# Operand addresses, two interleaved projections and the stored residual stream in a three-block kernel

## The chip, the cores and the metric

One NeuronCore of a Trainium2 chip runs the whole program. The metric is the device time of one execution in microseconds (us), as the median of several. TensorE is PE, VectorE is DVE, ScalarE is ACT, GpSimd is POOL, and SP issues most DMAs.

## The reference

Sequence 512, width 1024, float32. Two blocks run one after the other:

```
for layer in 0, 1:                                  # first block
    x += mixer(rmsnorm(x))                          # layer 0: stick-breaking + windowed heads; layer 1: latent attention
    x += swiglu(rmsnorm(x))                         # hidden 2816
x = rmsnorm(x, final_norm)
proj = rms_norm(x, ln_attn_pre) @ w_in              # second block
mix  = concat(rwkv7_mix(proj[:, :1792]), diff_attention(rest))
h = x + rms_norm(mix @ w_out)
h = h + rms_norm((gelu(conv gate) * conv val) @ w_down)
```

The product `rms_norm(x) @ w_in`, with x already the normed output of the first block, is where two of the three edits are. The second block later needs this normed x again, as the residual h.

## The kernel before

Activations lie transposed: eight tiles x0 to x7 of 128 channels by 512 tokens. Each float32 operand of a product is cut into a rounded high part and a low part (`whi`, `wlo` for weights, `xh`, `xl` for activations; `h`, `l`, `ah`, `al`, `t` in the swiglu). `mm3` makes three matmuls of them, high by high, high by low, low by high; ACT makes the high part, DVE the low one. A matmul streams its second operand against the weights loaded for it, and the weights of the next matmul are loaded beside it. The widths streamed are 512 columns, or 256 in the swiglu's gate and up products (`product`, L721), which are combined from half-size blocks.

**Where tiles lie.** The pools stand one after the other in each partition's memory. Constants end at byte 18,080, which leaves 32 modulo 128. The weight pool `wp` (raw, whi, wlo) and the activation pool `xp` (x, xh, xl) begin there, and all their tiles are multiples of 128 long, so each starts at 32 modulo 128. The work pool `wk` and all pools of a stage (attention, swiglu `ff`, second block) start at 0. The pools on the right-hand side, `po` (weights of the output projection) and `ffr` (a swiglu's extra weight tiles), start at 96. In the swiglu the weight parts rotate over three places, two in `wp` and one in `ffr`; half of the activation blocks `t` lie in `ff`, half in `xp`.

**Order.** In the swiglus the order of PE, DVE, ACT and SP is written out by hand. In the second block only PE's order is; the other engines' order is made by a planner that goes by traced order and simulated readiness.

**Start of the second block.** `bridge` makes xh and xl of each x tile once the last swiglu has added to it, and two sums of squares on ACT and POOL. PE then does the first projection (24 matmuls), the sums (`norms`, L1081), the second projection, a third, and the broadcast of the norm `rbc` (L248). `norms` also gives the vector `rf` from which the residual stream is made: `keep(ks)` multiplies x by the gain on ACT, by the broadcast norm `rkv` on POOL (L1072), and stores it to DRAM over ACT's queue (L1073), to be read back much later. The table `SLOTS` says after which half projection of which head pair t each step stands; `keep:0123` stands in the last slot of t = 0, beside `norm1` (a reciprocal root by Newton steps on tiny tiles, L228 to L234, then the ACT copy `rnb`, L1192). `late` is `norm2`, whose first step on PE is `pnb` (L1199), in the middle of the next projection. The buffers x0 to x7 are taken over by the tiles `lms` in t = 1 and t = 2.

Of the kernel before, what the change touches and what calls it, by code (L numbers as in the profile page):

```python
# [8 lines left out]
F32 = mybir.dt.float32  # L9
F32R = mybir.dt.float32r  # L10
I32 = mybir.dt.int32
AF = mybir.ActivationFunctionType
ALU = mybir.AluOpType
# [69 lines left out]
class Net:  # L83
    def __init__(self, tc, A, stack, dbg=None):
        self.tc, self.nc, self.A, self.dbg = tc, tc.nc, A, dbg or {}
        nc = self.nc
        self.cst = stack.enter_context(tc.tile_pool(name="cst", bufs=1))
        self.wp = stack.enter_context(tc.tile_pool(name="wp", bufs=3))
        self.xp = stack.enter_context(tc.tile_pool(name="xp", bufs=1))
        self.sm = stack.enter_context(tc.tile_pool(name="sm", bufs=2))  # L90
        self.wk = stack.enter_context(tc.tile_pool(name="wk", bufs=2))
        self.cv = self.cst.tile([128, A["cv"].shape[1]], F32, name="cv")
        nc.sync.dma_start(out=self.cv, in_=A["cv"])
        self.tables()
        self.ident = self.cst.tile([128, 128], F32, name="ident")
        self.ones = self.cst.tile([128, 128], F32, name="ones")
        nc.vector.memset(self.ones, 1.0)
        self.x = [self.xp.tile([128, S], F32, tag=f"x{k}", name=f"x{k}") for k in range(NT)]
        self.acc = None
        self.pb = [self.pool(stack, f"p{i}", n, PSUM) for i, n in enumerate((2, 3, 2, 1))]  # L100


    def banks(self, *ids):
# [399 lines left out]
    def project_out(self, banks, w, oh, ol, cut):  # L503
        v_, g_ = self.nc.vector, self.nc.gpsimd
        for m in range(8):
            ps = banks[0][0].tile([128, S], F32, tag=banks[0][1], name="pso")
            self.dense(ps, [self.A[w][m][:, :cut * 128]], oh, ol)
            v_.tensor_tensor(out=self.x[m], in0=self.x[m], in1=ps, op=ALU.add)
        edge = Edge(self)
        with self.tc.tile_pool(name="po", bufs=1, side="right") as pw, self.tc.manual_schedule(engines={mybir.EngineType.PE}):  # L510
            n, ws, jobs = 1024 - 128 * cut, [], []

            def part(m, ps, c, ks):
                for k in ks:
                    o = slice(128 * (k - cut), 128 * (k - cut) + 128)
                    self.mm3(ps, *[w[:, o] for w in ws[m]], oh[k][:, c], ol[k][:, c], k == cut, k == 7)

            for i, c in enumerate(HALVES):
                for m in range(8):
                    p_, n_ = banks[(8 * i + m) % len(banks)]  # L520
                    ps = p_.tile([128, S], F32, tag=n_, name="pso")[:, 0:256]
                    if not i:
                        ws.append([pw.tile([128, n], F32R, name=f"w{j}{m}") for j in "hl"])
                        self.chunk(self.A[w][m][:, cut * 128:], g_ if m in PJL else None, None, ws[m])
                    jobs.append((m, ps))
                    part(m, ps, c, range(cut, 7))

                    if not i and m < PJW:
                        continue
                    for m_, ps in jobs:  # L530
                        part(m_, ps, c, (7,))
                        v_.tensor_tensor(out=self.x[m_][:, c], in0=self.x[m_][:, c], in1=ps, op=ALU.add)
                        edge.squares(m_, i)
                    jobs = []
                    if i and m == PJN[0]:
                        edge.norm(0)
                    if i and m == PJN[1]:
                        edge.spread(0)
        return edge
# [186 lines left out]
    def ffn(self, i, edge):  # L726
        nc, A = self.nc, self.A
# [4 lines left out]
        with ExitStack() as st:  # L732
            pp = self.pool(st, "ff", 1)
            w2 = self.pool(st, "ffw", 1)
            pw = st.enter_context(self.tc.tile_pool(name="ffr", bufs=1, side="right"))
            pg = self.banks(*FFB[i])
            place = lambda n: pp.tile([128, 4, 256], F32R if n != "y" else F32, tag="a", name=n, bufs=8)
# [7 lines left out]


            y, T = [place("y") for _ in range(4)], {}

            def scaled(q):
                c = HALVES[q // 2]  # L750
# [39 lines left out]
            p1, s1, m5, u, pa, pb, cs, hq, hr, done, ws, sm, quads = ({} for _ in range(13))  # L790
# [165 lines left out]
            def ahead(n):  # L956
# [3 lines left out]
                if n + 1 < len(jobs):  # L960
# [7 lines left out]
            turn = {2: lambda: quadrant("B12", 2), 3: lambda: quadrant("B22", 3),  # L968
                    4: lambda: term("T1", lambda: y[2], lambda: y[0]), 6: lambda: term("T2", lambda: y[3], lambda: t["T1"]),
                    8: lambda: term("T3", lambda: y[3], lambda: y[2]), 13: lambda: term("T4", lambda: y[1], lambda: t["T2"])}  # L970
# [63 lines left out]
    def bridge(self, psp):  # L1034
        nc = self.nc
        gg = self.sm.tile([128, 8], F32, name="gg", bufs=1)
        nc.vector.tensor_tensor(out=gg, in0=self.col("final_norm", 0, 8), in1=self.col("ln_pre", 0, 8), op=ALU.mult)
        xh = [self.xp.tile([128, S], F32R, tag=f"xh{k}", name=f"xh{k}") for k in range(NT)]
        xl = [self.xp.tile([128, S], F32R, tag=f"xl{k}", name=f"xl{k}") for k in range(NT)]
        acc2 = self.sm.tile([128, S], F32, tag="rq", name="acc2", bufs=1)  # L1040
        for k in range(NT):
            self.prep(k, self.x[k], gg[:, k:k + 1], xh[k], xl[k])
            gf = self.col("final_norm", k)
            if k == 0:
                nc.scalar.activation(out=acc2, in_=self.x[k], func=AF.Square, scale=gf)
            else:
                t = self.wk.tile([128, S], F32, tag="sqt", name="sqt")
                nc.scalar.activation(out=t, in_=self.x[k], func=AF.Square, scale=gf)
                nc.gpsimd.tensor_add(out=acc2, in0=acc2, in1=t)
        got = {}  # L1050

        def norms():
            ps = psp.tile([128, S], F32, tag="r", name="pss")
            _, vf = self.meansq(psp, D, 1e-6, ps=ps[:, 0:4])
            self.acc = acc2
            v2, _ = self.meansq(psp, D, 0.0, ps=ps[:, 4:8])
            rf = got["rf"] = self.rsqrt(vf, [128, 4], "rf", FAST[1])
            nc.vector.tensor_tensor(out=v2, in0=v2, in1=rf, op=ALU.mult)
            nc.vector.tensor_tensor(out=v2, in0=v2, in1=rf, op=ALU.mult)
            nc.vector.tensor_scalar(out=v2, in0=v2, scalar1=1e-6, scalar2=None, op0=ALU.add)  # L1060
            r2 = self.rsqrt(v2, [128, 4], "r2", FAST[1])
            nc.vector.tensor_tensor(out=r2, in0=r2, in1=rf, op=ALU.mult)
            return r2


        def keep(ks):
            if ks[0] == 0:
                got["b"] = self.bcast(psp, got["rf"], "rkv")
                self.hsp = self.A["scratch"].tile([NT, 128, S], F32, tag="hsp", name="hsp", bufs=1)
            for k in ks:  # L1070
                nc.scalar.activation(out=self.x[k], in_=self.x[k], func=AF.Copy, scale=self.col("final_norm", k))
                nc.gpsimd.tensor_tensor(out=self.x[k], in0=self.x[k], in1=got["b"], op=ALU.mult)  # L1072
                nc.scalar.dma_start(out=self.hsp[k], in_=self.x[k])  # L1073
        return xh, xl, norms, keep

    def meansq(self, psp, dim, eps, tag="r", ps=None):
# [17 lines left out]
    def block2_attn(self):  # L1094
        nc, A = self.nc, self.A
        v_, g_, s_, t_ = nc.vector, nc.gpsimd, nc.scalar, nc.tensor
        with ExitStack() as st:
            pp = self.pool(st, "ba", 1)
# [5 lines left out]
            xh, xl, norms, keep = self.bridge(pr)  # L1104
# [34 lines left out]
            def bank(name="psr"):  # L1139
                p_, n_ = banks[npb[0] % 4]  # L1140
                npb[0] += 1
                return p_.tile([128, S], F32, tag=n_, name=name)
# [177 lines left out]
                        {"norm1": norm1, "norm2": norm2, "decays": decays}[n_](t)  # L1320

            with self.tc.manual_schedule(engines={mybir.EngineType.PE}):
                first = [bank(), bank()]
                for m in range(2):
                    self.dense(first[m], [A["w_in2"][m]], xh, xl)
                    if m == 0:
                        rc = norms()
                kr = [bank(), bank()]
                self.dense(kr[0], [A["w_in2"][6]], xh, xl)
                rbc = self.bcast(pr, rc, "rbc")  # L1330
# [102 lines left out]
            with self.tc.manual_schedule(engines={mybir.EngineType.PE}):  # L1433
# [18 lines left out]
                for hh in range(2):  # L1452
                    ps = ((pg, pv)[hh]).tile([128, 4, 4, 32], F32, tag="go"[hh], name="psi")
# [4 lines left out]
                for hh in range(2):  # L1458
                    ps = pc.tile([128, 4, 4, 32], F32, tag="c", name="psi2")
# [507 lines left out]
def constants():  # L1967
# [57 lines left out]
LAG = (2, 3)  # L2025
WP = ()

SLOTS = [["", "", "", "", "decays", "norm1 next keep:0123"],
         ["late keep:45", "turn:v keep:67", "", "within:0 within:1 norm1", "turn:bh bonus", "turn:kh within:2 within:3 next"],
         ["late", "turn:v", "", "within:0 within:1", "within:2 within:3 bonus", "turn:bh turn:kh"]]  # L2030
CUT = (5, 5)
NEWT = 1
# [25 lines left out]
```

## Time and profile before

| | us |
|---|---|
| median of 3 runs (lowest, highest) | 2031.12 (2030.57, 2034.69) |
| profiled execution | 2029.36 |
| its span | 2027.7 |
| PE busy | 1931.1 |
| DVE busy | 1350.5 |
| ACT busy | 896.7 |
| POOL busy | 428.7 |

Busy time is the time in which an engine had an instruction under way; consecutive matmuls overlap, so a matmul's own duration is longer than the distance to the next one's start. The first swiglu's products begin at 293 us, the latent attention's projections at 661 us, the second swiglu's products at 905 us, the second block's at 1269 us, those of its own feed-forward part at 1649 us.

### The profile page before, as it was taken

Reading aid. Unit: us, or ns where it says so; the run is one execution under the profiler, and the core shown is the slowest. Engines: PE = TensorE matmul, PEld = TensorE weight load, DVE = VectorE, ACT = ScalarE, POOL = GpSimd, SP = SyncE. Lnnn points to the kernel's source line nnn. Section 1 sums busy time; section 2 is a strip of 40 time slices with the busy share of each in tenths; the row PEclk is TensorE's granted clock in tenths of the full one; section 3 lists DMA queues with packets and bytes.
Section 4 is the critical chain, followed back from the end, with each engine's and each line's share of the span. In section 5 each row is a group of like instructions: output and inputs, shape, how many; then the busy total and the mean of one; then the engine's idle time right before and its main releaser. Section 6 shows DMA issues by size and latency. Waiting matters only on the chain. (4 is left out here: it accounts for less than half of the span.)

```text
span 2027.7 us, 29686 instructions
## 1 busy us (share of the span) xinstructions
PE 1931.1 (95%) x11652; PEld 1646.6 (81%) x11652; DVE 1350.5 (67%) x2287; ACT 896.7 (44%) x1538; POOL 428.7 (21%) x429
## 2 busy tenths in 40 slices
PE   9999988999999999998999999889899999999997
PEld 8766788999997777778999998668687788888886
DVE  6555568777767666567867676777958578666324
ACT  5454454444344555445434445534146445444321
POOL 2434210000002265320000002354333242111001
PEclk9998998999999999999999999989999999999998
DMA  4210142323323210033323132222111112223232
GB/s 161 99 58 7 32 155 94 128 71 117 100 75 96 73 49 27 28 116 105 123 86 132 66 104 77 84 89 69 63 53 45 62 58 98 95 94 100 89 95 70
DMA packets 58123, 169.56 MB, mean 84 GB/s; under 512 B 6304, under 2 KB 13504, under 8 KB 57984
## 3 DMA queue, kind: packets, MB, share of 16 engines
q1 hardware_dynamic: 54672, 162.70, 24.5%
q10 hardware_dynamic: 3232, 4.72, 0.7%
q8 instruction: 91, 1.49, 0.3%
q14 instruction: 48, 0.39, 0.1%
q0 software_dynamic: 80, 0.26, 0.0%
HBM read 161.89 MB, written 5.77 MB: 83 GB/s over the span
## 5 line engine op out<-in xcount | busy, mean ns | idle before, releaser
L168 ACT CAST whi<-raw 128x1024 fp32r<-128x1024 f32 (+3 forms) x146 | 144.4, 991 | 286.9 <-PE o L175 93.6
L169 DVE TENSOR_TENSOR wlo<-raw,whi 128x1024 fp32r<-128x1024 f32 (+3 forms) x138 | 163.4, 1184 | 129.6 <-ACT whi L168 129.0
L721 PE MATMUL pa<-t,h 128*128 128x256 f32 x960 | 177.3, 286 | 10.4 <-DVE u L895 8.4
L1029 POOL TENSOR_TENSOR acc<-acc,sqt 128x256 f32<-128x256 f32 (+1 forms) x58 | 69.3, 1194 | 486.2 <-ACT sqt L1028 484.5
L721 PEld LDWEIGHTS pa<-t,h 128*128 128x128 f32 x960 | 152.1, 193 | 12.8 <-ACT ah L846 8.8
L207 DVE TENSOR_TENSOR l<-r,h 128x1024 fp32r<-128x1024 f32 x104 | 127.0, 1222 | 52.1 <-ACT h L206 52.1
L721 PE MATMUL pa<-t,l 128*128 128x256 f32 x480 | 137.2, 286 | 2.2 <-DVE l L207 2.2
L206 ACT CAST h<-r 128x1024 fp32r<-128x1024 f32 x104 | 107.8, 1046 | 67.1 <-PE pd L175 20.5
L175 PE MATMUL o<-xl,whi 128*128 128x512 f32 (+1 forms) x352 | 134.6, 383 | 2.1 <-DVE xl L214 2.1
L174 PE MATMUL o<-xh,whi 128*128 128x512 f32 (+1 forms) x352 | 134.8, 383 | 0.0
L176 PE MATMUL o<-xh,wlo 128*128 128x512 f32 (+1 forms) x352 | 134.0, 381 | 0.0
L176 PE MATMUL pd<-ah,l 128*128 128x512 f32 x320 | 126.8, 396 | 2.0 <-DVE l L207 2.0
L174 PE MATMUL pd<-ah,h 128*128 128x512 f32 x320 | 126.7, 396 | 0.3 <-ACT h L206 0.3
L175 PE MATMUL pd<-al,h 128*128 128x512 f32 x320 | 126.6, 396 | 0.0
L721 PE MATMUL p<-t,h 128*128 128x256 f32 x640 | 119.0, 286 | 4.1 <-ACT h L206 4.1
L721 PE MATMUL pb<-t,h 128*128 128x256 f32 x640 | 115.7, 281 | 0.0
L721 PEld LDWEIGHTS p<-t,h 128*128 128x128 f32 x640 | 101.6, 193 | 5.9 <-ACT h L206 4.6
L721 PEld LDWEIGHTS pb<-t,h 128*128 128x128 f32 x640 | 99.4, 190 | 1.0
L206 ACT CAST h<-raw 128x768 fp32r<-128x768 f32 (+2 forms) x76 | 62.3, 820 | 85.5 <-PE pd L175 60.9
L721 PEld LDWEIGHTS pa<-t,l 128*128 128x128 f32 x480 | 93.0, 194 | 3.0 <-DVE l L207 3.0
L721 PE MATMUL p<-t,l 128*128 128x256 f32 x320 | 91.7, 287 | 3.0 <-DVE l L207 3.0
L721 PE MATMUL pb<-t,l 128*128 128x256 f32 x320 | 90.4, 283 | 0.5 <-DVE l L207 0.5
(549 smaller groups left out, 5337.1 us busy)
## 6 DMA issues: line engine op xcount, KB each, us to landing
r<-w_gu SPq DMA_DIRECT2D x88, 512.0 KB, 3.5
raw<-w_gu SPq DMA_DIRECT2D x56, 512.0 KB, 3.5
raw<-w_dn SPq DMA_DIRECT2D x48, 384.0 KB, 4.1
raw<-w_in SPq DMA_DIRECT2D x22, 512.0 KB, 3.4
raw<-w_dn SPq DMA_DIRECT2D x16, 448.0 KB, 3.2
raw<-w_qka SPq DMA_DIRECT2D x8, 512.0 KB, 3.5
raw<-w_dn SPq DMA_DIRECT2D x16, 256.0 KB, 2.6
raw<-w_out SPq DMA_DIRECT2D x8, 512.0 KB, 3.5
```

The lines of the kernel that those rows point to most:

```text
L168: nc.scalar.copy(out=hi[:, :n], in_=raw[:, :n])
L169: (eng or nc.vector).tensor_sub(out=lo[:, :n], in0=raw[:, :n], in1=f(hi[:, :n]))
L174: mm(out, lh, rh, start=start, stop=False)
L175: mm(out, lh, rl, start=False, stop=False)
L176: return mm(out, ll, rh, start=False, stop=stop)
L206: self.nc.scalar.copy(out=hi, in_=src)
L207: (eng or self.nc.vector).tensor_sub(out=lo, in0=src, in1=f(hi))
L721: self.nc.tensor.matmul(c, l, r, start=first and n == 0, stop=k == 3 and n == 2, skip_group_check=True)
L1029: return nc.gpsimd.tensor_add(out=self.acc[:, c], in0=self.acc[:, c], in1=t)
```

## The change

Unused tiles are put in (each filled once on POOL, since a tile has to be written): 96 bytes ahead of `wp`, 32 bytes behind `wk`, 32 bytes on the right ahead of `po` and of `ffr`, and 64 bytes in `ff` behind the tiles `a` (which hold ah, al) and ahead of the blocks `t`. By the sums of the sizes, `wp` and `xp` then start at 0 modulo 128, `wk` at 96, `po` and `ffr` at 64, the `t` tiles of `ff` and the pool `ffw` behind them at 64, and all else stays at 0. The first two projections of the second block are done for k = 0 to 6 of both, then k = 7 of both, and `norms` stands behind the second instead of behind the first. `keep` becomes one DVE instruction a tile, held behind the DVE instruction traced just ahead of it (pinned), with the store of tile k-1 pinned on ACT behind the work on tile k; the tiles are spread over seven slots of t = 0 and t = 1.

```diff
+        self.gap(stack, "gap0", 16512 + -(-4 * A["cv"].shape[1] // 32) * 32 + 2 * 512, 0)
         self.wp = stack.enter_context(tc.tile_pool(name="wp", bufs=3))
...
         self.wk = stack.enter_context(tc.tile_pool(name="wk", bufs=2))
+        self.gap(stack, "gap1", 96, 0)
...
+    def gap(self, stack, name, at, to, side="left"):
+        n = (to - at) % 128 // 4
+        if n:
+            p_ = stack.enter_context(self.tc.tile_pool(name=name, bufs=1, side=side))
+            self.nc.gpsimd.memset(p_.tile([128, n], F32, name=name), 0.0)
...
+        self.gap(right, "gap2", 64, 96, "right")
...
+            self.gap(st, "gap3", 64, 96, "right")
...
+            nc.gpsimd.memset(pp.tile([128, 16], F32, name="gap4"), 0.0)
...
             for k in ks:
-                nc.scalar.activation(out=self.x[k], in_=self.x[k], func=AF.Copy, scale=self.col("final_norm", k))
-                nc.gpsimd.tensor_tensor(out=self.x[k], in0=self.x[k], in1=got["b"], op=ALU.mult)
-                nc.scalar.dma_start(out=self.hsp[k], in_=self.x[k])
+                pin(nc.vector.scalar_tensor_tensor(out=self.x[k], in0=self.x[k], scalar=self.col("final_norm", k), in1=got["b"], op0=ALU.mult, op1=ALU.mult))
+                if k:
+                    pin(nc.scalar.dma_start(out=self.hsp[k - 1], in_=self.x[k - 1]))
+            if k == 7:
+                pin(nc.scalar.dma_start(out=self.hsp[7], in_=self.x[7]))
...
                 first = [bank(), bank()]
-                for m in range(2):
-                    self.dense(first[m], [A["w_in2"][m]], xh, xl)
-                    if m == 0:
-                        rc = norms()
+                ws = [self.chunk(A["w_in2"][m]) for m in range(2)]
+                for ks in (range(7), (7,)):
+                    for ps, (hi, lo) in zip(first, ws):
+                        for k in ks:
+                            c = slice(k * 128, k * 128 + 128)
+                            self.mm3(ps, hi[:, c], lo[:, c], xh[k], xl[k], k == 0, k == 7)
+                rc = norms()
...
-SLOTS = [["", "", "", "", "decays", "norm1 next keep:0123"],
-         ["late keep:45", "turn:v keep:67", "", "within:0 within:1 norm1", "turn:bh bonus", "turn:kh within:2 within:3 next"],
+SLOTS = [["", "", "", "", "decays", "norm1 next keep:01"],
+         ["late keep:2", "turn:v keep:3", "keep:4", "within:0 within:1 norm1 keep:5", "turn:bh bonus keep:6", "turn:kh within:2 within:3 next keep:7"],
```

## Rows read from the trace of the kernel before

**Rows 1.** The page: head, and part 1 (busy time, share of the span, instructions).
```profile
span 2027.7 us, 29686 instructions
...
PE 1931.1 (95%) x11652; PEld 1646.6 (81%) x11652; DVE 1350.5 (67%) x2287; ACT 896.7 (44%) x1538; POOL 428.7 (21%) x429
```

**Rows 2.** Waits of PE, longest in total: us in total, times, longest.
```profile
PE pnb L1199 <- ACT rnb L1192: 11.3, 1, 11.3
...
PE psr L175 <- DVE xl L214: 3.8, 1, 3.8
```

**Rows 3.** Groups of PE instructions by form: count, busy us, mean ns, idle before.
```profile
L174 PE MATMUL pd<-ah,h 128*128 128x512 f32 x320 | 126.7, 396 | 0.3 <-ACT h L206 0.3
...
L174 PE MATMUL o<-xh,whi 128*128 128x512 f32 x320 | 124.8, 390 | 0.0
```

**Rows 4.** PE's timeline, start and duration in us: six unbroken runs, first and last.
```profile
357.07 0.40 PE L721 MATMUL pa<-t,h 128*128 128x256 f32 x2
...
359.78 0.28 PE L721 MATMUL pa<-t,l 128*128 128x256 f32 x1
...
380.73 0.40 PE L174 MATMUL pd<-ah,h 128*128 128x512 f32 x1
...
384.69 0.40 PE L176 MATMUL pd<-ah,l 128*128 128x512 f32 x1
...
457.00 0.40 PE L721 MATMUL pb<-t,h 128*128 128x256 f32 x2
...
459.75 0.28 PE L721 MATMUL pb<-t,l 128*128 128x256 f32 x1
...
1011.02 0.40 PE L721 MATMUL p<-t,h 128*128 128x256 f32 x2
...
1013.74 0.28 PE L721 MATMUL p<-t,l 128*128 128x256 f32 x1
...
1601.53 0.40 PE L176 MATMUL o<-my,wk 128*128 128x512 f32 x1
...
1606.60 0.40 PE L174 MATMUL o<-my,wk 128*128 128x512 f32 x1
...
1752.01 0.39 PE L174 MATMUL o<-xh,whi 128*128 128x512 f32 x1
...
1763.80 0.39 PE L175 MATMUL o<-xl,whi 128*128 128x512 f32 x1
```

**Rows 5.** Timelines of POOL, DVE, ACT and PE around PE's longest wait, and a later Newton step.
```profile
1315.26 10.79 POOL L1072 TENSOR_TENSOR x<-x,rkv 128x512 f32<-128x512 f32 x8
...
1313.33 0.17 DVE L228 TENSOR_SCALAR rsb<-n 128x8 int32<-128x8 int32 x1
...
1318.78 1.19 DVE L232 TENSOR_TENSOR rst<-rsy 128x8 f32<-128x8 f32 x1
...
1326.11 0.62 ACT L1192 COPY rnb<-rsy 128x512 f32<-128x512 f32 x1 [8.35 <-DVE rsy L234]
...
1326.78 2.08 PE L1199 MATMUL pnb<-ident,rnb 128*128 128x128 f32 x8 [11.26 <-ACT rnb L1192]
...
1345.07 0.17 DVE L232 TENSOR_TENSOR rst<-rsy 128x8 f32<-128x8 f32 x1
```

**Rows 6.** Timeline, PE and DVE, at the start of the second block.
```profile
1269.08 0.39 PE L174 MATMUL psr<-xh,whi 128*128 128x512 f32 x1
...
1274.69 2.73 DVE L1116 TENSOR_SCALAR c<-cv 128x2 f32<-128x2 f32 x4
...
1277.34 1.21 DVE L169 TENSOR_TENSOR wlo<-raw,whi 128x1024 fp32r<-128x1024 f32 x1
1278.47 0.74 DVE L214 SCALAR_TENSOR_TENSOR xl<-x,gg,xh 128x512 fp32r<-128x512 f32 x1
...
1297.40 0.48 PE L174 MATMUL psr<-xh,whi 128*128 128x512 f32 x1
```

**Rows 7.** One stretch: PE, PEld, DVE, ACT, POOL busy (instructions), granted clock, DMA.
```profile
1315.00:1332.00 17.00, 5.74 (x20) 4.59 (x19) 13.69 (x15) 1.88 (x3) 11.77 (x10) 0.60 0.23 86
```

More of the change, by code (lines that the diff above doesn't have):

```diff
@@ L509, in project_out @@
         edge = Edge(self)
-        with self.tc.tile_pool(name="po", bufs=1, side="right") as pw, self.tc.manual_schedule(engines={mybir.EngineType.PE}):
+        right = ExitStack()
+        self.gap(right, "gap2", 64, 96, "right")
+        with right, self.tc.tile_pool(name="po", bufs=1, side="right") as pw, self.tc.manual_schedule(engines={mybir.EngineType.PE}):
             n, ws, jobs = 1024 - 128 * cut, [], []
@@ L1066, in keep @@
         def keep(ks):
+            pin = self.tc.keep_in_program_order
             if ks[0] == 0:
```

## The prediction

> **What bounds the kernel now.** I read the page's head first: PE is busy 1931.1 of 2027.7 us, 95% [rows 1]. So two things can be won: less time per matmul, and PE's idle 97 us. The second view, PE's waits, shows where the idle time is: the largest single one is `pnb` waiting 11.3 us for the ACT copy `rnb`, and `psr` waits 3.8 us for an `xl` [rows 2]; both stand in the stretch that two of the three edits touch. The third view, PE's groups by form, gives the first: two groups of 320 matmuls of the same shape, with the same partners on the other engines, last 396 ns (`pd<-ah,h`) and 390 ns (`o<-xh,whi`) on the mean [rows 3]. The fourth, PE's timeline in unbroken runs, shows that this is the distance from one start to the next. Where weights and streamed operand both start at 32 modulo 128 (xh, xl against whi, wlo), 52 steps take 1763.80 - 1752.01 = 11.79 us, 226.7 ns each; where the stream starts at 0 and the weights at 32 (ah, al against a part in `wp`), 17 steps take 3.96 us, 232.9 ns [rows 4]. The starts modulo 128 come from the sums of the tile sizes.
>
> **Part one, the padding.** What counts in it is the distance, modulo 128, between the streamed tile and the weights. I go by class, 512 columns first.
>
> Pairs now 32 or 96 apart that come to lie 0 apart: two thirds of the 960 `pd` matmuls (weights rotate over two places in `wp` and one in `ffr`), 640; the last product of the kernel 7 x 66 = 462; the latent attention's projections from ch 240; the second block's output projection 96; together about 1,438. What a pair at 0 and 0 costs is shown by one run only, `o<-my,wk`, 5.07 us for 22 steps, 230.5 ns [rows 4], in a stage with many short pieces; the long run with both at 32 has 226.7. The gain per pair lies between 2.4 and 6.2 ns; I take 4.5, the middle, since most of these pairs stand in long runs but the directly equal row is the dearer: -6.5 us (-3.5 to -8.9).
>
> Pairs that stay 0 apart and move from 32 and 32 to 0 and 0: by the counts 3 x 320 (xh, xl in the feed-forward part) and some 1,320 more in the projections, about 2,280. Nothing if only the distance counts, and that is my value; if they all cost what the one run at 0 and 0 costs, +3.8 ns each, +8.7 us. The 320 `pd` matmuls with weights on the right go from 96 to 64 apart, for which no run of this width is quoted here: between 0 and -6.2 ns by the two runs above, +-2 us with the other sign allowed; I take -1.
>
> The 256-column products of the swiglus, 3,744 of them. Today's runs: 32 apart 2.72 us for 23 steps, 118.3 ns (`p`); 0 apart 119.6 (`pb`); 64 apart 117.8 (`pa`) [rows 4]. Blocks `t` in `ff` move from 0 to 64 and the weights from 32 to 0 or from 96 to 64: some 1,100 pairs go from 32 to 64 apart (-0.5 ns each, -0.6 us), some 600 from 96 to 0 apart (at most +1.3 ns, +0.8 us); those against `xp` keep their distance. I take +0.5 us.
>
> Part one: -6.5 - 1 + 0.5 = -7 us, spread over stages in which PE hardly waits, so nearly all of it shows. Bounds: -10.5 and, with the dear run for all 3,718 pairs, -3.5 + 8.7 = +5. `wk` moving to 96 is read by PE in a few dozen short matmuls only; nothing. The extra fills are a handful of tiny POOL instructions in stretches where POOL is mostly idle (429 of 2028 us busy, [rows 1]); nothing hangs on them; nothing.
>
> The Trainium skill's page "SBUF — State Buffer" states, in its section "SBUF: two separate sides", that on the engines' side only the pair of ports shared by VectorE and GpSimd is contended and that TensorE never waits on another engine, and its table under "A bandwidth-pool intuition that's wrong (but worth ruling out)" gives TensorE a second, independent read port for loading weights. By that, where weights and stream start should not matter, the part would be worth nothing, and the 396 against 390 ns would need another cause: rival (a) below. The rows make me side with the distance.
>
> **Part two, the residual stream on DVE.** PE reaches `pnb` at 1326.78 - 11.26 = 1315.5 us and gets it at 1326.78. In between POOL runs the eight multiplies of `keep`, 1315.26 to 1326.05, and DVE, which has nothing but the tiny Newton steps of `norm1` to do, does one per POOL instruction: 1.19 us a step where the same step later takes 0.17 [rows 5]. POOL's 10.79 us leave, so the chain runs at its own pace. It began at 1313.33 us; twelve steps at about 0.2 us (0.17 and the hand-over) are 2.4 us; what DVE interleaves with it anyhow (a shift and a scan, by the nearest rows 0.74 and 1.21 us [rows 6]) and the new multiplies come on top. A multiply of that shape with two operands in memory has its nearest row in `xl`, 0.74 us [rows 6]; beside a POOL instruction it can be held up by about 1 us (1.19 - 0.17). The pin of tile 0 is on the broadcast's diagonal, that of 1 on 0, that of 2 on a multiply of `norm2` that is done early, so the planner may put up to three of them, 2.2 us, into the chain. The copy `rnb` (0.62) follows [rows 5]. PE then restarts between 1317.0 and 1320.5 us; I take 1319.5, a wait of 4.0 instead of 11.3: -7.3 us.
>
> The granted clock was 0.60 in 1315 to 1332 us [rows 7], part of it at the 1.2 GHz level, after the wait began; the 8 rows of `pnb` took 2.08 us [rows 5]. PE did 20 instructions in 5.74 busy us there, against some 3.7 at 2.4 GHz by estimate (12 x 0.227 and half of 2.08): 2 us lost. A wait of 4 us may still drop the clock; I count 1.2 back. Part two: -8.5 us, between -5.5 and -11.
>
> The other five multiplies stand on DVE in t = 1: 5 x 0.75 = 3.7 us in a stretch in which PE is the fuller engine; each lies behind a traced neighbour and ahead of nothing that PE needs within the same half projection. I take +0.5 us, between 0 and +3 (each held up by POOL once). ACT loses eight scalings, which cover nothing. The eight stores stay on ACT's queue; each now waits for a tile finished one step earlier except the last, behind which ACT's next weight cast is queued; the stores land well ahead of `lms` in the same buffers, a slot or more later: nothing.
>
> **Part three, the interleaving.** From the first `psr` at 1269.08 to the third projection's successor at 1297.40 PE needs 28.3 us [rows 6] for 72 matmuls (16.4 us at 0.227) and the small sums and broadcast (about 3 by estimate): 9 us are lost to waits and the lower clock. Now 21 matmuls of the second projection stand ahead of the one that needs the last `xl`, 4.8 us of work against the 3.8 us wait. But they need the second `wlo`, and DVE begins it only at 1277.34, behind tiny constants (four of them 2.73 us) and just ahead of `xl` at 1278.47 [rows 6]. If the planner leaves that order, PE stops about 3 us at `wlo` instead of 3.8 at `xl`; if it moves `wlo` up, because its cast is traced earlier and ACT has less to do, the wait goes. `norms` comes one projection later; its chain (some 25 tiny steps of 0.2, 5 us) now lies beside one projection (5.5 us) instead of two, just enough. I take -3 us, between +1 and -6.
>
> **The sum.** -7 - 8.5 + 0.5 - 3 = -18 us. The profiled execution was 2029.36 us (span 2027.7 and 1.7 around it), 1.8 below the median of 2031.12; 2029.4 - 18 = 2011.4, and on the median's footing 2013.
>
> **Rivals.** (a) Offsets are worth nothing: only parts two and three, -11: 2020 us. For it: the three runs stand in three stages with different company; against it: 226.7, 230.5 and 232.9 ns come in the order of the distances. (b) A pair at 0 and 0 costs 230.5 ns everywhere: part one +5, sum -6: 2025. For it: the only equal run; against it: that run stands among short pieces. (c) DVE takes POOL's place: the multiplies sit in the chain and are themselves held up by POOL, and PE still waits 9 us: part two -2.5, sum -12: 2019. For it: the pins are one-sided; against it: POOL has little left to do there. (d) Slower: what makes 226.7 is that both operands start at 32, not that they are equal. Then 2,280 pairs go to 232.9 (+14.1), none of the 1,438 gains, and the 256-column pairs 64 apart go from 117.8 to 119.6 (860 pairs, +1.6): +15.7 against -11, +4.7: 2036. It decides from a step above 226.7 + 11/2.28 = 231.5 ns for pairs at 0 and 0. The run of 230.5 lies just below that.
>
> **How the numbers follow.** Chances: forecast 0.55, (a) 0.13, (b) 0.12, (c) 0.13, (d) 0.07. The forecast's own range is 2006 to 2019; to leave no more than 2 in 10 outside, the range runs from 2003 to 2026, which holds (a), (b) and (c) with a little beyond the forecast's lower end. About 0.2%, 4 us, is what a measurement of this kernel can tell from no change. Faster by more: the forecast, (a), (c) and nearly all of (b), 0.89; within: the rest of (b) and half of (d), 0.06; slower: 0.05.
>
> **What would show it.** Part one: runs of `pd` and of the last product at 227 to 230 ns a step instead of 233, and xh against whi unchanged at 227; if those go above 231, (d). Part two: no POOL multiply of x, Newton steps near 0.2 us, a wait at `pnb` of 2 to 5 us; 9 would be (c). Part three: the wait at `xl` gone, perhaps one at `wlo`, and the fourth projection's start less than 28 us behind the first's. Wrong overall if the time is above 2026.

## The result and the profile after

The changed kernel takes 2018.39 us (median of 5 runs, 2018.19 to 2025.36) where the kernel before took 2034.45 beside it: a ratio of 0.9943, 95% interval 0.9928 to 0.9959. A second set of six gave 2020.76 and 0.9947 (0.9931 to 0.9963). The medians of the first set lie 16 us apart, but three of its five runs of the kernel before were among the slowest; over all runs on record the means are 2020.1 (11 runs) and 2031.1 (49 runs). So the change is worth 11 us (7 to 15). The forecast was 2013, its range 2003 to 2026: direction and range held, the sum of 18 us was 7 too large. The time alone doesn't tell the forecast from its rivals (a), 2020, and (c), 2019; the runs of the parts do.

The execution whose profile is shown is the slowest of the five, 2025.36 us. Its page, head and part 1, beside [rows 1]:

```profile
span 2023.6 us, 29687 instructions
...
PE 1934.1 (96%) x11652; PEld 1655.3 (82%) x11652; DVE 1348.1 (67%) x2295; ACT 892.2 (44%) x1530; POOL 420.5 (21%) x429
```

PE's busy time has not fallen: a matmul at half clock is busy for longer, and this execution has more half clock than that of the kernel before (118 us against 107 in the records). So the parts have to be read where they act. **Padding**, PE's groups by form, beside [rows 3]:

```profile
L184 PE MATMUL pd<-ah,h 128*128 128x512 f32 x320 | 125.6, 392 | 0.3 <-ACT h L216 0.3
L184 PE MATMUL o<-xh,whi 128*128 128x512 f32 x320 | 124.8, 390 | 0.0
```

PE's timeline, first and last of four unbroken runs, beside [rows 4]:

```profile
1011.37 0.39 PE L184 MATMUL pd<-ah,h 128*128 128x512 f32 x1
...
1015.26 0.39 PE L186 MATMUL pd<-ah,l 128*128 128x512 f32 x1
...
1039.12 0.40 PE L733 MATMUL p<-t,h 128*128 128x256 f32 x2
...
1041.83 0.28 PE L733 MATMUL p<-t,l 128*128 128x256 f32 x1
...
1054.64 0.39 PE L184 MATMUL pd<-ah,h 128*128 128x512 f32 x1
...
1058.54 0.39 PE L186 MATMUL pd<-ah,l 128*128 128x512 f32 x1
...
1680.20 0.39 PE L185 MATMUL o<-xl,whi 128*128 128x512 f32 x1
...
1886.49 0.39 PE L186 MATMUL o<-xh,wlo 128*128 128x512 f32 x1
```

`pd` with both operands at 0 takes 3.90 us for 17 steps, 229.4 ns (the run that starts at 1054.64), and with the weights 64 away 3.89 us, 228.8 (1011.37); before it was 232.9. `p`, now 64 apart, has 2.71 us for 23 steps, 117.8 (118.3). The fourth run is 910 steps of xh and xl against whi and wlo in 206.29 us, 226.7 ns, the same as before the move from 32 and 32 to 0 and 0.

**Residual stream**, the timelines of DVE, ACT and PE around `pnb`, beside [rows 5]:

```profile
1313.40 0.17 DVE L244 SCALAR_TENSOR_TENSOR rsy<-rst,rsy 128x8 f32<-128x8 f32 x1
1313.48 1.41 DVE L1087 SCALAR_TENSOR_TENSOR x<-x,cv,rkv 128x512 f32<-128x512 f32 x2
1314.81 0.16 DVE L242 TENSOR_TENSOR rst<-rsy 128x8 f32<-128x8 f32 x1
1314.88 1.41 DVE L1087 SCALAR_TENSOR_TENSOR x<-x,cv,rkv 128x512 f32<-128x512 f32 x2
...
1317.32 0.62 ACT L1210 COPY rnb<-rsy 128x512 f32<-128x512 f32 x1 [2.69 <-DVE rsy L244]
...
1317.99 2.08 PE L1217 MATMUL pnb<-ident,rnb 128*128 128x128 f32 x8 [5.42 <-ACT rnb L1210]
```

POOL's row of 10.79 us is gone, a Newton step takes 0.17 us, and the wait is 5.42 us. Four multiplies, 2.8 us, stand among the Newton steps. `pnb` still takes 2.08 us and the matmuls behind it start 0.43 us apart, at half clock: this lasts until 6.2 us after the start of `pnb`, where it was 5.0 us before, so the shorter wait gave no clock back here.

**Interleaving**, PE's waits from 1258 to 1330 us, beside [rows 2, 6]:

```profile
PE pnb L1217 <- ACT rnb L1210: 5.4, 1, 5.4
PE psr L186 <- DVE wlo L179: 1.6, 1, 1.6
PE pss L1099 <- DVE v L1102: 0.9, 1, 0.9
```

The wait at `xl` is gone, and PE doesn't stop at the second `wlo`: it stops 1.6 us at the first. The fourth projection starts 22.5 us behind the first one's start (1271.95 and 1294.42 us; 28.3 before). Not all of this is the interleaving's. DVE's tiny constants ahead of the second `wlo`, 2.73 us before [rows 6], take

```profile
1277.24 0.61 DVE L1134 TENSOR_SCALAR c<-cv 128x2 f32<-128x2 f32 x4
...
1277.87 2.25 POOL L1044 TENSOR_TENSOR acc<-acc,sqt 128x512 f32<-128x512 f32 x1 [0.79 <-ACT sqt L1043]
```

0.61 us, while POOL waits 0.79 us between two additions. Before, POOL was adding nearly all the while:

```profile
1274.62 1.29 POOL L1029 TENSOR_TENSOR acc<-acc,sqt 128x512 f32<-128x512 f32 x1
...
1275.87 1.26 POOL L1049 TENSOR_TENSOR acc<-acc,sqt 128x512 f32<-128x512 f32 x1
```

The runs of the parts below show which edit does this.

Now the stretches between fixed points of PE's program, in us, in three profiled executions:

| stretch | before | after | after, second profile |
|---|---|---|---|
| both feed-forward parts from the first `pd` on, and the last product from `o<-ah` on | 676.3 | 670.7 | 669.2 |
| first `psr` to `pnb` | 57.7 | 46.0 | 46.1 |
| both feed-forward parts up to the first `pd` | 198.1 | 203.0 | 199.9 |
| the chain (first `pxy` to `psg`) | 95.3 | 101.1 | 101.1 |
| the rest | 1000.2 | 1002.9 | 1003.7 |
| span | 2027.7 | 2023.6 | 2019.9 |

The first two lines are 17 to 19 us better, what was forecast; 11 to 13 are given back elsewhere. The third line is partly chance: the first feed-forward part has 17.1 us of half clock there in the one profile and 6.8 in the other (10.2 before). The chain is not: it is 5.8 us longer in both profiles, and it begins 136 us after the last of the multiplies that were moved (1347.43 us). Of the rest, some 3 us are in the latent attention's output projection (26.1 and 26.5 us, 23.2 before), where PE waits 2.1 and 2.3 us for a sum from POOL (1.1 before) and half clock follows. No other kernel shown here has more than 23.6 us there, though the order on DVE, ACT and POOL there is that of the kernel before; the cause is open.

### The profile page after: what moved, and what is told of

Same layout as the page of the kernel before. It is cut to its first block, busy times and chain, and to the rows that moved or that the text cites. A ratio compares the mean times of both kernels' runs of the same rounds, so it can differ in the third digit from the quotient of the medians.

```text
span 2023.6 us, 29687 instructions
## 1 busy us (share of the span) xinstructions
PE 1934.1 (96%) x11652; PEld 1655.3 (82%) x11652; DVE 1348.1 (67%) x2295; ACT 892.2 (44%) x1530; POOL 420.5 (21%) x429
## 4 chain that ended last, share of the span: by engine, by line
PE 80%; DVE 13%; ACT 3%; issue 2%; DMA 1%; POOL 1%; SPq 0%; DVEq 0%; ACTq 0%; POOLq 0%
PE pa L733 8%; PE o L185 7%; PE o L184 6%; PE o L186 6%; PE pb L733 5%; PE p L733 4%; PE pd L186 4%; PE pd L184 4%; PE pd L185 4%; PE po L706 2%; PE t L698 1%; DVE l L217 1%; PE psq L184 1%; PE psq L185 1%; PE psq L186 1%
```

## Experiments

Each was timed against the kernel before.

**The three parts, each alone, and the opposite of the first.** The edits are the change's own hunks. The fourth puts 32 bytes between `wp` and `xp` and 96 behind `xp`, so that all else keeps its place modulo 128 (`shim` fills an unused tile of so many floats):

```
+        self.shim(stack, "gapA", 8)
         self.xp = stack.enter_context(tc.tile_pool(name="xp", bufs=1))
+        self.shim(stack, "gapB", 24)
```

Padding alone. 

> Only the padding (all five gaps); the second block as before. Theory (a matmul's step depends on how far, modulo 128 bytes, the tile that it streams lies from the weights of the next matmul: 512 columns 227.9 ns at 0, 230.0 at 64, 233.2 at 32, 233.9 at 96; 256 columns 119.5, 116.6, 118.3, 118.7, means of the two traces): 1,349 + 417 pairs of 512 columns leave 32 and 96, the 4,763 pairs of 256 columns go mostly to 0 and 64, and the sum over all pairs gives -9.8 us (-7 to -11), with the pnb wait at 11 us and the xl wait at 0.7 us as before. Rival (a), offsets are worth nothing: 0 +-2 us. Rival (b), a pair at 0 and 0 costs 230.5 ns wherever it stands: about -1 to +5 us.

Measured: 2024.38 us against 2031.35, ratio 0.997 (0.9959 to 0.9981), -6.1 us (-8 to -4). Rivals (a) and (b) are out. Two PE rows of its trace:

```profile
473.86 0.40 PE L184 MATMUL pd<-ah,h 128*128 128x512 f32 x1
...
481.82 0.39 PE L186 MATMUL pd<-ah,l 128*128 128x512 f32 x1
```

35 steps, 227.4 ns. The waits are those of the kernel before, 11.2 us at `pnb` and 3.8 at `xl` (the expectation's 0.7 doesn't fit [rows 2]). The gain is smaller than the pair sum: -9.8 lies outside the measured interval. In the three stretches of the table's first line, where PE hardly waits, the sum gives -7.7 and the profile -5.6, with 3.4 us of half clock in the first that the kernel before hasn't there, and 1.2 us less of it in the last. Corrected for that (half of 2.2 us), some 1 us of the sum is missing even there. Over 11 runs its mean granted clock is 0.973, as that of the kernel before over 22, so the faster steps are not paid for in clock. The other 2.1 us of the sum lie in stages in which PE waits for other engines as well; whether they are lost there was not tried.

Offset turned round. 

> The kernel before with 32 bytes put between the pools of the weights' split and of the streamed x (and 96 behind, so that everything after lies where it lay): the pairs that were 0 apart at (32, 32) become 32 and 96 apart. 512 columns: 2,341 pairs at 0 become 122, 2,523 at 96; 256 columns: 1,877 at 0 become 160. Theory (distance): the same sum over pairs gives +13.0 us (+10 to +16). Rival (a), offsets worth nothing: 0 +-2 us. Rival (d), what is fast is both at 32 and not the distance: as large a loss here, told apart only beside the padding run, which must then be slower too.

Measured: 2039.74, ratio 1.0051 (1.0037 to 1.0065), +10.4 us (+7.5 to +13). The run of 910 steps, same instructions, same neighbours:

```profile
1683.52 0.39 PE L181 MATMUL o<-xl,whi 128*128 128x512 f32 x1
...
1895.85 0.39 PE L182 MATMUL o<-xh,wlo 128*128 128x512 f32 x1
```

212.33 us, 233.3 ns a step instead of 226.7. With the padding run faster, this leaves the distance: with the starts of streamed tile and weights modulo 128 in brackets, (32, 32) and (0, 0) have 226.7, (0, 32) and (64, 32) 233. Rival (d) is out. Streamed tiles and weights were moved by pools, so whether it is the weights in use or the next ones, loaded beside them, that count was not separated. The Trainium skill's page "SBUF — State Buffer" (section "A bandwidth-pool intuition that's wrong (but worth ruling out)") gives TensorE's weight load an independent read port. The page says nothing of start addresses; whoever takes from it that they don't matter, as rival (a) does, is contradicted by these 910 steps, +6.6 ns each, and the measurement decides.

Residual stream alone. 

> Only the residual stream on VectorE in pinned instructions with its new slots; no padding, no interleaving. Theory: PE's wait at pnb goes from 11.3 to about 5 us, the Newton steps from 1.19 to 0.2 us, and with less half clock behind the wait the run is 6 to 8 us faster. Rival (the wait only moves on: VectorE's six later multiplies in t=1 delay the turned operands and PE waits there for as long): 0 to -2 us.

Measured: 2021.30, ratio 0.9961 (0.9947 to 0.9976), -7.9 us (-11 to -5). Its longest wait of PE in 1262 to 1330 us:

```profile
PE pnb L1202 <- ACT rnb L1195: 5.7, 1, 5.7
```

From the first `psr` to `pnb` 48.7 us instead of 57.7. Only 5.6 of these 9 us are the wait at `pnb`. The other 3.4 stand ahead of it, where no edit of this run is: the fourth projection starts 24.9 us behind the first one's start (28.3 before). VectorE's tiny constants there, and the wait at `xl` (3.8 before):

```profile
1273.35 0.61 DVE L1119 TENSOR_SCALAR c<-cv 128x2 f32<-128x2 f32 x4
```

```profile
PE psr L175 <- DVE xl L214: 1.6, 1, 1.6
```

All profiles with this edit have 0.61 us for the constants, all without it 2.7. So the time that the theory named holds, its account in part: the new order of the other engines does some of what the interleaving was to do. The rival of this run and (c) are out: VectorE's later multiplies cost PE nothing that shows (from `pnb` to the first `psd` PE takes 76.4 us, 77.0 before).

Interleaving alone. 

> Only the two first projections interleaved and the norms behind them; residual on GpSimd, no padding. Theory: the way from the first projection's first instruction to the fourth projection falls from 28.3 to about 22.5 us and all that follows comes that much earlier: -4 to -6 us. Rival (the gain is given back at pnb, because GpSimd's multiplies of the residual begin behind the norms, which now come later than the projections): the wait at pnb grows from 11.3 to 14 us or more, and the run is 0 to -2 us.

Measured: 2029.49, ratio 0.9992 (0.9981 to 1.0004), -1.6 us (-4 to +1). PE's waits in 1258 to 1330 us:

```profile
PE pnb L1199 <- ACT rnb L1192: 11.1, 1, 11.1
PE psr L176 <- DVE wlo L169: 3.8, 2, 2.9
PE pss L1081 <- DVE v L1084: 0.9, 1, 0.9
```

Neither theory: the wait at `pnb` doesn't grow, but the gain isn't there to give back. The 3.8 us at `xl` [rows 2] have become 2.9 at the second `wlo`, which still stands behind the slow constants:

```profile
1271.49 2.73 DVE L1116 TENSOR_SCALAR c<-cv 128x2 f32<-128x2 f32 x4
```

The fourth projection starts 27.6 us behind the first one's start, not 22.5; first `psr` to `pnb` is 56.8 us, 0.9 less. The way to the fourth projection is thus 28.3 us before, 24.9 with the residual stream's edit, 27.6 with the interleaving, and 22.5 with both.

**Where the rest of the sum went.** The parts alone add up to -15.6 us, together they give -11. With the errors of four measurements (some 5 us) this difference alone isn't clear of noise; the comparison below, with one part taken out, is.

The changed kernel again. 

> The changed kernel once more, with a new profile, timed beside the others of this call. If the extra stretches of half clock in its first profile (118 us against 107 before; the run took 2025.36 us, its other four 2018.2 to 2019.0) are chance, this profile has them elsewhere or not at all and the median stays at 2018 +-2 us. If the faster steps of the padding bring them about, the same stretches (first product of both feed-forward blocks, the chain before psg) are at half clock again.

Measured: 2020.76, 0.8 above the expected bound. Both answers, by stretch: the half clock at the start of the first feed-forward part was chance; that of the second part (13.7 us in both profiles, 10.2 before; 10.2 to 17.1 in the kernels below) and of the chain is the same twice. The chain as a stretch, with busy times (instructions) of PE, PEld, DVE, ACT, POOL, then the granted clock, the DMA share and GB/s; first profile:

```profile
1484.20:1585.30 101.10, 96.10 (x884) 78.30 (x882) 75.43 (x278) 52.39 (x133) 28.96 (x30) 0.92 0.13 43
```

the second profile:

```profile
1480.50:1581.60 101.10, 96.09 (x883) 78.32 (x882) 75.44 (x278) 52.42 (x133) 29.00 (x30) 0.92 0.13 43
```

and the same stretch of the next kernel, the changed one without its interleaving:

```profile
1478.50:1574.90 96.40, 92.32 (x881) 76.03 (x881) 75.25 (x278) 52.57 (x133) 29.85 (x30) 0.95 0.14 45
```

The same work on every engine, at 0.92 against 0.95 of the clock. That kernel's edit to the changed one:

```
-                ws = [self.chunk(A["w_in2"][m]) for m in range(2)]
-                for ks in (range(7), (7,)):
...
-                rc = norms()
+                for m in range(2):
+                    self.dense(first[m], [A["w_in2"][m]], xh, xl)
+                    if m == 0:
+                        rc = norms()
```

> The changed kernel without the interleaving (padding and residual stream kept). Theory: the interleaving is worth what it was alone, 1 to 2 us, so this is 0 to +2 us against the changed kernel. Rival: it is worth more in company, since no GpSimd multiply stands at pnb any more to take back what the bridge gives: +3 to +6 us against the changed kernel, with a wait at xl of 1.6 us or more and one at the second product's weights gone.

Measured: 2014.98, ratio 0.9927 (0.9911 to 0.9942); by the means of 6 and 11 runs 4.1 us (1.3 to 6.9) faster than the changed kernel. Both theories are wrong in sign. Padding and residual stream add up within the noise: -14.8 us together, -14.0 by the two runs alone. From the first `psr` to `pnb` it has 48.7 us, 2.7 more than the changed kernel; the chain has 96.4, 4.7 less. The latent attention's output projection has 23.3 us, 2.8 less, with a shorter wait for POOL's sum; PE's row in the changed kernel, then in this one:

```profile
PE sums L68 <- POOL acc L1044: 2.1, 1, 2.1
```

```profile
PE sums L68 <- POOL acc L1044: 0.7, 1, 0.7
```

These three make the measured 4 us and a little more. In the chain, VectorE's timeline in the changed kernel:

```profile
1559.22 1.22 DVE L179 TENSOR_TENSOR wk<-raw,wk 128x1024 fp32r<-128x1024 f32 x1
...
1560.74 0.69 DVE L254 TENSOR_TENSOR dg<-ident,rsy 128x512 f32<-128x512 f32 x1
1561.35 0.41 DVE L1495 COPY xs<-pxy 64x256 f32<-64x256 f32 x1
```

and this one:

```profile
1552.24 1.22 DVE L179 TENSOR_TENSOR wk<-raw,wk 128x1024 fp32r<-128x1024 f32 x1
1553.38 0.41 DVE L1492 COPY xs<-pxy 64x256 f32<-64x256 f32 x1
```

PE's row that waits for `xs`, in the changed kernel:

```profile
1561.81 1.15 PE L1503 MATMUL pu<-xs,TT 64*64 64x64 f32 x16 [1.58 <-DVE xs L1495]
```

and in this one:

```profile
1553.85 1.14 PE L1500 MATMUL pu<-xs,TT 64*64 64x64 f32 x16 [0.63 <-DVE xs L1492]
```

No line of the chain differs between the two kernels, but the order that the planner gives VectorE there does: a `dg` and four small Newton steps have slipped ahead of `xs`. PE waits 1 us longer, and the chain holds 17.1 us at half clock instead of 9.6: 7.5 us at half speed, 3.8 lost. Of these 7.5 us, one stretch of 3.4 follows this wait, another 3.4 lie some 14 us later. Why so short a wait brings so much half clock was not settled, and no run changed this order alone: that it costs the 4.7 us is read from the traces, not shown.

**Taking more of the wait.** Two edits of the slots in the changed kernel, first the late multiplies, then the early norm as well:

```
-SLOTS = [["", "", "", "", "decays", "norm1 next keep:01"], ["late keep:2", "turn:v keep:3", "keep:4",
...
+SLOTS = [["", "", "", "", "decays", "norm1 next"], ["late", "turn:v keep:012", "keep:34",
...
+SLOTS = [["", "", "", "norm1", "decays", "next"], ["late", "turn:v keep:012", "keep:34",
...
```

Late multiplies. 

> The changed kernel with the first three multiplies of the residual moved from the slots around pnb to the middle of the next tile's r projection, so that none of them stands among the Newton steps. Theory (four of them, 2.8 us, hold up the Newton steps on VectorE, and PE waits 5.4 us at pnb): the wait falls to about 2.6 us, the run is 2 to 4 us faster than the changed kernel. Rival (other work of VectorE takes their place in the chain, and the wait is set by what pn waits for): the wait stays at 5 us, 0 +-1 us.

Measured: 2014.20, ratio 0.992 (0.9903 to 0.9937), by the means 5.7 us faster than the changed kernel beside it (2020.4). The gain is larger than the theory's and comes by another way: the wait fell to 3.9 us, 1.5 less and not 2.8, while the chain has 95.1 us, 6.0 less, although the interleaving is in. A wait of 1.8 at `psa` has grown from 0.8. PE's waits in 1258 to 1330 us, then in 1318 to 1345:

```profile
PE pnb L1217 <- ACT rnb L1210: 3.9, 1, 3.9
```

```profile
PE psa L1186 <- DVE lms L1286: 1.8, 1, 1.8
```

In this chain Newton steps stand ahead of `xs` too, but `dg` is behind it, and PE waits 0.9 us for `xs`, not 1.6. VectorE there:

```profile
1550.06 0.41 DVE L1495 COPY xs<-pxy 64x256 f32<-64x256 f32 x1
...
1550.80 0.68 DVE L254 TENSOR_TENSOR dg<-ident,rsy 128x512 f32<-128x512 f32 x1
```

Early norm. 

> As the run before, and the norm of the first tile (norm1 of t=0) is issued one slot earlier, behind the r projection instead of behind the v projection, so that its Newton steps run while PE has the v projection. Theory: the wait at pnb is gone (below 0.5 us) and with it most of the 6.8 us of half clock behind it: 6 to 9 us faster than the changed kernel, at about 2011 us. Rival (what the norm leaves behind is held up elsewhere: decays of the same tile come later on VectorE and ScalarE, and the next wait is for them or for bh): half of it is taken back, 2 to 4 us.

Measured: 2015.89, ratio 0.9922 (0.9909 to 0.9936). By the means that is 5.3 us faster than the changed kernel beside it, between theory and rival. The wait at `pnb` is gone, and part of it comes back elsewhere, as the rival said, though not for `decays` or `bh`: 3.4 us for `lms`, whose multiply on VectorE stands behind two of those of x, and 1.6 us at `pn`. PE's waits in 1258 to 1345 us:

```profile
PE psa L1186 <- DVE lms L1286: 3.4, 1, 3.4
PE psr L186 <- DVE wlo L179: 1.6, 1, 1.6
PE pn L1205 <- ACT kk L1202: 1.6, 1, 1.6
```

Late multiplies without the interleaving. 

> Padding and residual stream on VectorE, without the interleaving (as in the run that took 2014.98 us), and with the first three multiplies moved to the middle of the next tile's r projection. Theory (the two changes add up: the wait at pnb falls from 5.6 to about 3.9 us and the chain before psg stays at 95 to 96.5 us): 2012 us (2010 to 2014). Rival (what the late multiplies save at pnb they take back at psa of the next tile, or VectorE's order in the chain becomes that of the changed kernel, 101 us): 2015 us or more.

Measured: 2015.36, ratio 0.992 (0.9907 to 0.9933): the rival's figure, and its first reason is in the trace (1.8 us at `psa`; the chain has 95.4, the wait at `pnb` 4.1). The interval of the ratio, +-2.6 us, reaches the theory's range as well, so the two are not told apart by the time. With late multiplies the interleaving is worth nothing that can be measured: 2014.20 with it, 2015.36 without.

Norm half a slot early, all eight multiplies in the next r projection, no interleaving:

```
+SLOTS = [["", "", "", "", "norm1 decays", "next"], ["late", "turn:v keep:0123", "keep:4567",
...
```

> As the run before, with the norm of the first tile issued in the middle of the v projection, ahead of the decays (one half slot earlier), and all eight multiplies of the residual in the two slots of the next tile's r projection. Theory: PE waits under 1.5 us at pn and pnb together and not at psa, 2009 us (2006 to 2012). Rival (eight multiplies in a row, 5.9 us of VectorE, hold up the eviction of the r projection, so that PE stands at psr or pslm for some us): 2014 us or more.

Measured: 2012.61, ratio 0.9913 (0.9896 to 0.9929), the lowest of all. 0.9 us at `pn`, none at `pnb`, but 1.9 at `pbon` and 1.5 at `psa`, both for `lms`: between theory and rival. By the means of 6 and 11 runs it beats the changed kernel by 6.6 us (3.3 to 9.9); it isn't told apart from the other kernels with late multiplies.

## Why the prediction was right, and where it was not

- **What bounds.** Right: PE's step and PE's waits were the two things to win.
- **Padding, -7.** Right: -6.1 alone. The guess of 4.5 ns a pair, for want of a long run at 0 and 0, was low: the means of all pairs of 512 columns outside the half clock are 228.0 ns at 0 (3,560 pairs after), 233.2 at 32 and 233.9 at 96 (before), 5 to 6 ns. The 230.5 of `o<-my,wk`, on which (b) stood, was a row of a stage in short pieces, as the prediction suspected. That nearly all of the sum shows was not borne out: the steps got 10 us shorter, the kernel 6. So -7 was met by a gain per pair that was too low and a share of it that was too high, which is in part luck.
- **Residual stream, -8.5 + 0.5.** The number is right, -7.9 alone, and the mechanism at `pnb` too, but not the terms. The wait came out at 5.4 to 5.7 us, not 4.0: the prediction's own terms, with all three multiplies, add up to 5.0, and a fourth went into the Newton chain (0.7). Of the 1.2 us for the clock, the changed kernel shows none and the run alone some 0.8 (half clock for 3.5 us from the start of `pnb`, 5.0 before). What made up for both is a term that the prediction hadn't: 3.4 us ahead of `pnb`, where the constants and the `xl` behind them come earlier. That the number was met is luck to this extent. The other four multiplies, in t = 1, cost nothing seen beyond 0.8 us at `psa`.
- **Interleaving, -3.** Its place was right (a wait at `wlo` for that at `xl`), its size alone too large: -1.6 (-4 to +1), not told apart from nothing. In company the bridge gained 2.7 us, but the kernel without it is faster.
- **The sum.** The step that failed was adding the parts as if what stands behind them stayed as it was. An edit can change the planner's order up to the end of the block. In the chain the changed kernel is 5.8 us longer than the kernel before, and some 3 us longer in the latent attention's output projection, from a cause that is open. With padding and residual stream alone the sum holds (-14.8 us); the interleaving, which was to give 3, takes 4 back. Nothing in the trace of before could price that, and no rival had it.
- **Rivals.** (a) is out by -6.1 alone and 233.3 against 226.7; (b) by 228.0; (c) by a wait of 5.4 and not 9; (d) by 226.7 at 0 and 0. All four are out by these, not by the total, to which (a) and (c) came nearer than the forecast.

## What to carry to other kernels

Where two products of one shape differ by a few ns a step, look at where streamed tile and weights begin, and check by moving one pool and nothing else. When a planner orders the engines, a gain in one stretch must be booked on the whole span: compare every later stretch, those without an edit above all. When work is moved to another engine, look for what stands in that engine's queue on the way to the next wait: put behind that wait, the multiplies cost less here, but some of the gain came back as a wait for what then stood behind them.

## What the hardware showed that was not expected

For 256 columns the distance matters too, but not in the same order: means of 119.4 to 119.6 ns at 0, 116.0 to 117.8 at 64, 118.3 to 119.1 at 32, and at 96 118.7 in the kernel before but 116.9 in the one with the pools 32 apart. The range is 3 ns, and what else decides was not found. For 512 columns 64 apart costs 229.8 (after, 410 pairs), 1.8 more than 0, but not wherever it occurs: some matmuls of `pd` that stream `a` took 229.6 at (96, 32) before and take 233.4 at (64, 0) now (48 and 44 pairs). So the distance is not all that counts there.
